# Hybrid encoder layer on one core: the sums of w_o planned behind the first output products, three more warm-up products, another transfer rate for the norm row

## The chip, the cores and the metric

The kernel runs on one core of a Trainium2 chip. The core has a matrix engine (TensorE, "PE" in the profile, with its weight loads as "PEld"), a vector engine (VectorE, DVE), a scalar engine (ScalarE, ACT), a general engine (GpSimd, POOL) and an engine that here only issues transfers (SyncE, SP). Each engine works through its own list of instructions in order; semaphores make one wait for another. The metric is the time on the device, in microseconds, of one execution; lower is better. Inputs and outputs lie in HBM.

## The reference

One layer over 512 tokens of width 1024, all in float32. Two sub-layers, each normed before and after:

```python
h = rmsnorm(x, pre_mix_norm)
proj = h @ w_in                       # z, x/B/C, dt, q, k, v, gates
y_ssd  = ssd_branch(z, xbc, dt, ...)  # conv, two scans, gated norm, @ w_ssd_out
y_attn = window_attention(q, k, v, sink, rel_table) @ w_attn_out
mixed = (g_ssd * y_ssd + g_attn * y_attn) @ w_o
x = x + rmsnorm(mixed, post_mix_norm)
f = square(relu(rmsnorm(x, pre_mlp_norm) @ w_mlp_in)) @ w_mlp_out
x = x + rmsnorm(f, post_mlp_norm)
```

The scan runs forward and backward over 8 groups of 4 heads, in chunks of 128 tokens. Its result is gated by silu(z), and normed within each group of 256 channels before `w_ssd_out` (2048 x 1024).

## The kernel before

**Arithmetic.** A float32 product is made of three faster ones: each operand is split into a high part `wh` (a cast on ACT) and a low part `wl` (source less high part, on POOL or DVE), and PE adds high by high, high by low and low by high. `mm3` issues the three. Weights come in chunks of 8 x 128 rows by 128 columns: SP fetches a chunk into `wr` (three buffers), ACT makes `wh` (three buffers), POOL `wl` (three buffers).

**Stages, in the order of the program.** A start of warm-up products on zeros (`WARM`), a broadcast of the first norm's gain by a one-row product (`pp<-g,one`), the norms and transposes of x, and the products for v and dt; then q, k, the gates, the eight scan groups (`ssd_quanta`, `ssd_steps`) with attention in between; then the output projection of the scan (`ssd_out_quanta`), the mix with w_o (`mix_quanta`), and the MLP.

**The turn from the scan to its output projection.** For the last group, `rms` sums the squares over partitions with two products against ones (operands `sh` and `sl`, the high and low part of the squares `ssq`), copies one row of the result (`rstd`), and sends it through HBM: row out (`rrow<-rstd`), back in as a column (`rcol<-rrow`), a power on POOL (`rsqrt_mean`, L383 and L385), out again (`rrow<-rcol`), and back as a row on all partitions (`rstd<-rrow`). DVE then makes the last two blocks of `yT` (L1179), which are split into `yh` and `yl` like the fourteen others (`split_y`, L1225 and L1226; eight of these lie in the tiles named `b`). `ssd_out_quanta` begins with the first fourteen blocks of y for the output columns 0 and 1 (`most`), and takes blocks 14 and 15 later (`rest`).

**The sums of w_o.** The mix is a product by halves in seven block products instead of eight, which needs sums of quarters of w_o. `stage_wo(k)`, for k from 0 to 3, fetches four tiles of w_o (L1341, tiles `wd`), makes four sums on DVE (L1344 to L1347) and stores them in HBM (L1349, tensors `wot`), from where the mix fetches them again (L1547). Here it is placed at the first quanta of the output projection: `c0 + STAGE + k` with STAGE at 0.

**What sets the order.** The program is written quantum by quantum (a quantum is one group of products, with side work put to it by `at`). At the end `chain` gives all instructions to `Planner`, which plays them through with durations of its own: an engine that is free takes, among the instructions that are ready, the one with the earliest deadline (PE the one that comes first in the program). The deadline of an instruction goes back from the PE instructions that need it. The order that comes out, engine by engine and for SP's transfers too, is fixed. `transfer` gives the planned length of a transfer by a rate for each source, and `COLD` the planned time up to which PE runs at half its pace. So a number in the planner moves instructions, and an engine in its fixed order waits where the plan was wrong.

Of the kernel before, what the change touches and what calls it, by code (L numbers as in the profile page):

```python
# [27 lines left out]

LO_MIX = "vp"
LO_DOWN = "p", "p", "p", "vp"  # L30
WARM = 10
LO_V = "pvpvpvpv"

SCAN = dict(load=3, weigh=(-2, -0.5), states=(0, 1), prep=(0, 1.5, 3, 4.5), outs=(2.5, 5.5), rms=9, finish=12,
            x_flip=2, b_flip=2)
LAST = dict(SCAN, prep=(0, 1, 3, 4), outs=(2.5, 5.5), rms=8, finish=10)
HEADS = dict(scores=0, flip=2, values=3.5)
FETCH, STAGE = 2, 0
BUCKET_STARTS = (1, 2, 3, 4, 5, 6, 7, 8, 12, 16, 23, 32, 46, 64, 91)


# [16 lines left out]
class Slots:  # L58


    def __init__(self, pool, n, tags):
        self.pool, self.free, self.slot, self.n, self.tags = pool, deque(range(n)), {}, 0, tags
# [14 lines left out]
class Planner:  # L77
# [10 lines left out]
    OVERLAP = {"ACT": 95, "DVE": 78, "POOL": 37, "PE": 0, "SP": 0}  # L88
    AFTER = {"ACT": 35, "DVE": 34, "POOL": 80, "PE": 53, "SP": 60}

    def __init__(self, instructions, tags):
        names = {"PE": "PE", "DVE": "DVE", "Activation": "ACT", "Pool": "POOL", "SP": "SP"}
        self.ins = [i for i in instructions if type(i).__name__ != "BassTilePoolBoundary"]
        self.eng = [names[str(i.engine).split(".")[-1]] for i in self.ins]
        self.tags = tags
        self.depend()
        self.cost = [self.duration(n) for n in range(len(self.ins))]
        self.kind = [self.matmul_kind(n) if e == "PE" else None for n, e in enumerate(self.eng)]

# [145 lines left out]
            late[n] = min([late[s] - self.AFTER[self.eng[s]] for s in self.post[n]] + [t + 5000.0]) - c  # L245
        return late

    COLD, LEAD, TAIL = 5300, 1000, 1300

    def transfer(self, n):  # L250

        dst, src = self.operands(self.ins[n].outs)[0], self.operands(self.ins[n].ins)[0]
        size = 4 * math.prod(d[1] for d in dst.ap)
        rows = {"csT": 120, "csE": 100, "in_w_in": 270, "in_w_mlp_in": 270, "in_w_ssd_out": 270, "in_w_attn_out": 270}
        return size / rows.get(src.tensor.name.rsplit("_", 1)[0] if src.tensor.name.startswith("cs") else src.tensor.name, 100 if size < 2 ** 17 else 310)

    def plan(self, wait=0.3):
        late = self.deadlines()
# [73 lines left out]
class Trunk:  # L332
    def __init__(self, ctx, tc, ins, out, dbg=None):
        self.tc, self.nc, self.out = tc, tc.nc, out
        self.__dict__.update({"d_" + k: v for k, v in ins.items()})
        self.d_w_in = ins["w_in"][0]
        self.dbg = dbg or {}
        pool = lambda name, **kw: ctx.enter_context(tc.tile_pool(name=name, bufs=1, **kw))
        self.cp = pool("cp")
        self.wp = pool("wp")  # L340
        self.sp = pool("sp")
        self.pm = pool("pm", space=PSUM)
        self.dp = pool("dp", space=DRAM)
        self.tags = {}
        self.slots = Slots(self.sp, SLOTS, self.tags)
        self.n = 0
        self.quanta, self.acts, self.now = [], {}, 0
        self.raw, self.parts, self.nraw, self.nspl, self.ring = {}, {}, 0, 0, set()

    def name(self, s):  # L350
# [138 lines left out]

    def chain(self):  # L490

        plan = Planner(self.nc.cur_bb.bb.instructions, self.tags)
        info = mybir.DependencyInfo(mybir.DependencyClass.NoSync, mybir.DependencyReason.DATA)
        for order in plan.plan().values():
            for a, b in zip(order, order[1:]):
                self.tc.add_manual_dep(plan.ins[b], plan.ins[a].name, info, reason="planned order")
# [823 lines left out]
    def load_x(self):  # L1320
# [7 lines left out]
        for t in range(NT):  # L1328
            self.x2[t] = [self.slots.get("x2") for _ in range(2)]
            for a, b in zip(self.x2[t], self.x1[t]):  # L1330
                self.nc.scalar.activation(a, b, AF.Copy, scale=self.rst0[:, t:t + 1])

    def stage_wo(self, k):

        nc = self.nc
# [309 lines left out]
    def build(self):  # L1645
# [6 lines left out]
        n = lambda: len(self.quanta)  # L1652
# [28 lines left out]
        c0 = n()  # L1681
        self.wot = {f"T{i}": self.dp.tile([512, 512], F32, name=f"wot{i}") for i in range(1, 5)}
        for k in range(4):
            self.at(c0 + STAGE + k, lambda k=k: self.stage_wo(k))
        self.at(c0, lambda: self.split_y(0, 14))
        self.add(*self.ssd_out_quanta())
        self.at(n() + 1, self.load_x)
# [44 lines left out]
```

## Time and profile before

| | us |
|---|---|
| runs shown (three): median, lowest, highest | 1089.49, 1088.82, 1089.90 |
| the profiled execution: its own time | 1092.5 |
| the profiled execution: its span | 1090.7 |

The page of the profile has the 40 slices of the span in these rows (busy tenths of each engine, granted PE clock, busy tenths of the DMA engines):

```profile
PE   9999999999999999999999999999999999999997
PEld 8788888888888888888888778888888888888885
DVE  5578887788796787886878863668863755665787
ACT  4567776686766768575677532475755534434443
POOL 3546567558558898999898866566998978978844
PEclk9999999999999999999999999999999999999999
DMA  6444524526435556555577964563721621621522
```

Each digit stands for 27 us. PE is at nine tenths or more up to the last slice; the other engines have room on the average. In the rows further on, "x <-y" in brackets behind an instruction says for how many us its engine stood idle before it, and what ended this; `L390` is the line of the helper `mm`, so that products are told apart by their tiles (`pp`, `ps` are banks of PSUM). "PEclk" is the granted clock as a share of the full one.

### The profile page before, as it was taken

What the parts mean: (1) busy time and instruction counts of PE and PEld (TensorE: products, weight loads), DVE (VectorE), ACT (ScalarE), POOL (GpSimd) and SP (SyncE); (2) the same over time, 40 slices, a digit from 0 to 9 for tenths busy, and PEclk for the clock granted to TensorE, in tenths of its full rate; (3) what the DMA queues carried; (4) which work ended last, traced back from release to release, by engine and by line L of the source; (5) the groups of instructions that cost most, each with busy time, mean ns of one, the idle gap of its engine ahead of it and who ended that gap; (6) DMA issues with size and microseconds to landing.
All of it is one profiled execution on the core that took longest, in us unless ns stands there. A gap on an engine that the chain in (4) does not pass through costs nothing.

```text
span 1090.7 us, 16951 instructions
## 1 busy us (share of the span) xinstructions
PE 1077.6 (99%) x5578; PEld 903.0 (83%) x5578; DVE 785.9 (72%) x1345; ACT 654.7 (60%) x1407; POOL 807.3 (74%) x1011
## 2 busy tenths in 40 slices
PE   9999999999999999999999999999999999999997
PEld 8788888888888888888888778888888888888885
DVE  5578887788796787886878863668863755665787
ACT  4567776686766768575677532475755534434443
POOL 3546567558558898999898866566998978978844
PEclk9999999999999999999999999999999999999999
DMA  6444524526435556555577964563721621621522
GB/s 204 127 124 121 152 75 121 147 67 164 128 112 159 152 144 164 156 150 163 141 188 207 284 176 134 162 225 112 246 66 53 191 69 52 192 65 57 161 93 78
DMA packets 221000, 152.21 MB, mean 140 GB/s; under 512 B 12494, under 2 KB 194230, under 8 KB 220913
## 3 DMA queue, kind: packets, MB, share of 16 engines
q1 hardware_dynamic: 220764, 151.06, 48.1%
q8 instruction: 44, 0.72, 0.3%
q14 instruction: 44, 0.35, 0.1%
q10 hardware_dynamic: 148, 0.07, 0.0%
HBM read 138.19 MB, written 12.91 MB: 139 GB/s over the span
## 4 chain that ended last, share of the span: by engine, by line
PE 92%; DVE 3%; DMA 2%; ACT 1%; issue 1%; POOL 0%; SPq 0%; POOLq 0%; DVEq 0%
PE pp L390 64%; PE ps L390 26%; PE ps L394 3%; DMA wr<-in_w_in 1%; DMA wd<-in_w_o 1%; DMA rstd<-rrow 1%; DVE wd L1345 0%; DMA rrow<-rcol 0%; ACT b L415 0%; DVE B L936 0%; DVE wd L1344 0%; DVE sl L408 0%; DVE x L1387 0%; DVE P L847 0%; DVE yT L1179 0%
## 5 line engine op out<-in xcount | busy, mean ns | idle before, releaser
L390 PE MATMUL pp<-b,wh 128*128 128x512 f32 (+1 forms) x1840 | 565.5, 388 | 0.2 <-DVE b L416 0.2
L469 POOL TENSOR_TENSOR wl<-wr,wh 128x256 fp32r<-128x256 f32 (+1 forms) x503 | 412.7, 849 | 140.0 <-ACT wh L465 129.9
L390 PEld LDWEIGHTS pp<-b,wh 128*128 128x128 f32 x1840 | 340.2, 188 | 67.9 <-issue 1.4
L390 PE MATMUL pp<-b,wl 128*128 128x512 f32 (+1 forms) x920 | 356.2, 387 | 0.0
L390 PEld LDWEIGHTS pp<-b,wl 128*128 128x128 f32 x920 | 172.8, 188 | 34.5
L465 ACT CAST wh<-wr 128x1024 fp32r<-128x1024 f32 x131 | 136.4, 1042 | 85.3 <-PE pp L390 68.0
L1561 POOL TENSOR_TENSOR wl<-wd,wh 128x256 fp32r<-128x256 f32 x168 | 139.3, 859 | 41.0 <-ACT wh L1557 35.2
L1557 ACT CAST wh<-wd 128x512 fp32r<-128x512 f32 x108 | 63.2, 618 | 55.0 <-PE pp L390 18.6
L390 PE MATMUL ps<-wh,fh 128*128 128x512 f32 (+1 forms) x196 | 75.5, 385 | 0.5 <-DVE acc L1607 0.5
L390 PE MATMUL ps<-wl,fh 128*128 128x512 f32 (+1 forms) x196 | 75.4, 385 | 0.0
L390 PE MATMUL ps<-wh,fl 128*128 128x512 f32 (+1 forms) x196 | 75.4, 385 | 0.0
L1104 ACT ACTIVATE n<-cb,tables 128x128 f32<-128x128 f32 x128 | 49.2, 391 | 18.2 <-DVE cb L1095 15.8
L1435 DVE SCALAR_TENSOR_TENSOR pp<-pp,r 128x512 f32<-128x512 f32 (+1 forms) x31 | 17.5, 566 | 56.0 <-ACT r L1432 55.9
L1561 POOL TENSOR_TENSOR wl<-wt,wh 128x256 fp32r<-128x256 f32 x56 | 45.4, 846 | 9.9 <-ACT wh L1557 6.0
L1140 POOL TENSOR_TENSOR w<-w,E 128x256 f32<-128x256 f32 x48 | 42.3, 893 | 11.8 <-DVE w L1136 5.4
L936 DVE SCALAR_TENSOR_TENSOR u<-pp,cv,u 128x510 f32<-128x510 f32 (+1 forms) x64 | 47.7, 745 | 3.4 <-ACT u L932 2.1
L1034 POOL TENSOR_TENSOR xd<-x,tables 128x256 f32<-128x256 f32 x48 | 35.5, 757 | 18.3 <-ACT x L959 16.0
L1105 ACT ACTIVATE m<-cb,tables 128x128 f32<-128x128 f32 x128 | 48.9, 388 | 0.0
L1100 ACT ACTIVATE rf<-rf,tables 128x128 f32<-128x128 f32 x128 | 42.4, 393 | 5.0 <-DMA rf<-csT 5.0
L390 PEld LDWEIGHTS ps<-wh,fh 128*128 128x128 f32 x196 | 36.8, 188 | 8.0 <-DVE acc L1607 0.7
L856 ACT ACTIVATE P<-P,mx 128x384 f32<-128x384 f32 (+1 forms) x64 | 35.2, 552 | 13.5 <-DVE mx L853 8.4
L390 PEld LDWEIGHTS ps<-wh,fl 128*128 128x128 f32 x196 | 36.8, 188 | 7.4
(301 smaller groups left out, 2094.5 us busy)
## 6 DMA issues: line engine op xcount, KB each, us to landing
wr<-in_w_in SPq DMA_DIRECT2D x74, 512.0 KB, 4.2
wr<-in_w_mlp_in SPq DMA_DIRECT2D x32, 512.0 KB, 4.1
wd<-in_w_mlp_out SPq DMA_DIRECT2D x64, 256.0 KB, 4.7
rb<-csT SPq DMA_DIRECT2D x32, 256.0 KB, 3.2
rf<-csT SPq DMA_DIRECT2D x32, 256.0 KB, 5.2
wd<-in_w_o SPq DMA_DIRECT2D x28, 256.0 KB, 4.7
wr<-in_w_ssd_out SPq DMA_DIRECT2D x14, 512.0 KB
E<-csE SPq DMA_DIRECT2D x96, 64.0 KB, 4.3
```

The lines of the kernel that those rows point to most:

```text
L390: self.nc.tensor.matmul(out, lhsT, rhs, start=start, stop=stop, skip_group_check=more)
L465: self.nc.scalar.copy(hi[:, :m], raw)
L469: engines[e].tensor_tensor(lo[:, c], raw[:, c], hi[:, c].bitcast(F32), op=ALU.subtract)
L856: nc.scalar.activation(p[:, :w], p[:, :w], AF.Exp, bias=mx[:, n:n + 1], accum_out=sm[:, n:n + 1])
L936: nc.vector.scalar_tensor_tensor(u[:, a:e], ps[:, a + d:e + d], self.wtap(t, b), u[:, a:e], op0=ALU.mult, op1=ALU.add)
L1034: nc.gpsimd.tensor_tensor(v4(xd[:, d * 256:(d + 1) * 256]), v4(xs(c)), by_dir(self.coef, c)[:, d].unsqueeze(2).to_broadcast([128, 4, 64]), ...
L1100: nc.scalar.activation(v4(rf)[:, h], v4(rf)[:, h], AF.Identity, bias=ncs[:, 0, h:h + 1])
L1104: nc.scalar.activation(v4(n)[:, h], cb[:, 0], AF.Copy, scale=dt[:, 0, h:h + 1])
L1105: nc.scalar.activation(v4(m)[:, h], cb[:, 1], AF.Copy, scale=dt[:, 1, h:h + 1])
L1140: nc.gpsimd.tensor_tensor(wc, wc, E[:, d], op=ALU.add)
L1557: nc.scalar.copy(hi, w)
L1561: (nc.vector if e == "v" else nc.gpsimd).tensor_tensor(low[:, q], w[:, q], hi[:, q].bitcast(F32), op=ALU.subtract)
```

## The change

It has three parts. `WARM` goes from 10 to 13 products, each of which is two PE instructions, and `COLD` from 5300 to 5600. STAGE goes from 0 to 1, and everything that `stage_wo` issues, its transfers too, is noted as held back: in the planner such an instruction may not begin before the PE instruction that stands last ahead of it in the program has begun. It is a rule for the plan alone; no semaphore is added. And transfers from `rrow` are planned at 70 instead of 100.

```diff
--- before.py
+++ after.py
@@ -28,14 +28,14 @@
 
 LO_MIX = "vp"
 LO_DOWN = "p", "p", "p", "vp"
-WARM = 10
+WARM = 13
 LO_V = "pvpvpvpv"
 
 SCAN = dict(load=3, weigh=(-2, -0.5), states=(0, 1), prep=(0, 1.5, 3, 4.5), outs=(2.5, 5.5), rms=9, finish=12,
             x_flip=2, b_flip=2)
 LAST = dict(SCAN, prep=(0, 1, 3, 4), outs=(2.5, 5.5), rms=8, finish=10)
 HEADS = dict(scores=0, flip=2, values=3.5)
-FETCH, STAGE = 2, 0
+FETCH, STAGE = 2, 1
 BUCKET_STARTS = (1, 2, 3, 4, 5, 6, 7, 8, 12, 16, 23, 32, 46, 64, 91)
 
 
@@ -88,12 +88,19 @@
     OVERLAP = {"ACT": 95, "DVE": 78, "POOL": 37, "PE": 0, "SP": 0}
     AFTER = {"ACT": 35, "DVE": 34, "POOL": 80, "PE": 53, "SP": 60}
 
-    def __init__(self, instructions, tags):
+    def __init__(self, instructions, tags, held=()):
         names = {"PE": "PE", "DVE": "DVE", "Activation": "ACT", "Pool": "POOL", "SP": "SP"}
         self.ins = [i for i in instructions if type(i).__name__ != "BassTilePoolBoundary"]
         self.eng = [names[str(i.engine).split(".")[-1]] for i in self.ins]
         self.tags = tags
         self.depend()
+        last = None
+        for n, i in enumerate(self.ins):
+            if self.eng[n] == "PE":
+                last = n
+            elif i.name in held:
+                self.turn[n].add(last)
+                self.next[last].append(n)
         self.cost = [self.duration(n) for n in range(len(self.ins))]
         self.kind = [self.matmul_kind(n) if e == "PE" else None for n, e in enumerate(self.eng)]
 
@@ -245,14 +252,14 @@
             late[n] = min([late[s] - self.AFTER[self.eng[s]] for s in self.post[n]] + [t + 5000.0]) - c
         return late
 
-    COLD, LEAD, TAIL = 5300, 1000, 1300
+    COLD, LEAD, TAIL = 5600, 1000, 1300
 
     def transfer(self, n):
 
         dst, src = self.operands(self.ins[n].outs)[0], self.operands(self.ins[n].ins)[0]
         size = 4 * math.prod(d[1] for d in dst.ap)
-        rows = {"csT": 120, "csE": 100, "in_w_in": 270, "in_w_mlp_in": 270, "in_w_ssd_out": 270, "in_w_attn_out": 270}
-        return size / rows.get(src.tensor.name.rsplit("_", 1)[0] if src.tensor.name.startswith("cs") else src.tensor.name, 100 if size < 2 ** 17 else 310)
+        rows = {"rrow": 70, "csT": 120, "csE": 100, "in_w_in": 270, "in_w_mlp_in": 270, "in_w_ssd_out": 270, "in_w_attn_out": 270}
+        return size / rows.get(src.tensor.name.rsplit("_", 1)[0].rstrip("01234567") if src.tensor.name.startswith(("cs", "rrow")) else src.tensor.name, 100 if size < 2 ** 17 else 310)
 
     def plan(self, wait=0.3):
         late = self.deadlines()
@@ -345,6 +352,7 @@
         self.slots = Slots(self.sp, SLOTS, self.tags)
         self.n = 0
         self.quanta, self.acts, self.now = [], {}, 0
+        self.late = set()
         self.raw, self.parts, self.nraw, self.nspl, self.ring = {}, {}, 0, 0, set()
 
     def name(self, s):
@@ -489,7 +497,7 @@
 
     def chain(self):
 
-        plan = Planner(self.nc.cur_bb.bb.instructions, self.tags)
+        plan = Planner(self.nc.cur_bb.bb.instructions, self.tags, self.late)
         info = mybir.DependencyInfo(mybir.DependencyClass.NoSync, mybir.DependencyReason.DATA)
         for order in plan.plan().values():
             for a, b in zip(order, order[1:]):
@@ -1330,6 +1338,12 @@
             for a, b in zip(self.x2[t], self.x1[t]):
                 self.nc.scalar.activation(a, b, AF.Copy, scale=self.rst0[:, t:t + 1])
 
+    def held_back(self, fn):
+
+        n = len(self.nc.cur_bb.bb.instructions)
+        fn()
+        self.late |= {i.name for i in self.nc.cur_bb.bb.instructions[n:]}
+
     def stage_wo(self, k):
 
         nc = self.nc
@@ -1681,7 +1695,7 @@
         c0 = n()
         self.wot = {f"T{i}": self.dp.tile([512, 512], F32, name=f"wot{i}") for i in range(1, 5)}
         for k in range(4):
-            self.at(c0 + STAGE + k, lambda k=k: self.stage_wo(k))
+            self.at(c0 + STAGE + k, lambda k=k: self.held_back(lambda: self.stage_wo(k)))
         self.at(c0, lambda: self.split_y(0, 14))
         self.add(*self.ssd_out_quanta())
         self.at(n() + 1, self.load_x)
```

What the planner makes of it is seen in three places. Lines of the changed kernel are 8 to 14 higher than before (L408 is L416 there, L1226 is L1234, L1344 to L1347 are L1358 to L1361, L445 is L453, L375 is L383).

On DVE, at the turn to the output projection. `wd` are tiles of w_o and their sums, `sl` is the low part of the last group's squares, `yl` and `b` are low parts of y. Before:

```order
L1226 TENSOR_TENSOR yl_7241<-yT_3605,yh_7240 128x512
L1345 TENSOR_TENSOR wd_7500<-wd_7494,wd_7492 128x512
L1347 TENSOR_TENSOR wd_7496<-wd_7496,wd_7500 128x512
L1344 TENSOR_TENSOR wd_7427<-wd_7431,wd_7427 128x512
L1345 TENSOR_TENSOR wd_7433<-wd_7427,wd_7425 128x512
L1347 TENSOR_TENSOR wd_7429<-wd_7429,wd_7433 128x512
L1346 TENSOR_TENSOR wd_7434<-wd_7431,wd_7433 128x512
L1344 TENSOR_TENSOR wd_7346<-wd_7350,wd_7346 128x512
L1226 TENSOR_TENSOR yl_7245<-yT_3608,yh_7244 128x512
L1345 TENSOR_TENSOR wd_7352<-wd_7346,wd_7344 128x512
L408 TENSOR_TENSOR sl_7121<-ssq_6934,sh_7120 128x512
L1226 TENSOR_TENSOR b_7230<-yT_5059,b_7228 128x512
```

In the changed kernel:

```order
L1234 TENSOR_TENSOR yl_7230<-yT_3611,yh_7229 128x512
L1234 TENSOR_TENSOR yl_7238<-yT_4451,yh_7237 128x512
L1144 TENSOR_TENSOR w_6510<-ps_7103,w_6510 128x512
L416 TENSOR_TENSOR sl_7124<-ssq_6937,sh_7123 128x512
L1234 TENSOR_TENSOR b_7215<-yT_5062,b_7213 128x512
L1234 TENSOR_TENSOR b_7215<-yT_5065,b_7213 128x512
```

and, behind the eight splits into `b`, in the changed kernel:

```order
L1234 TENSOR_TENSOR b_7216<-yT_6896,b_7214 128x512
L1358 TENSOR_TENSOR wd_7331<-wd_7335,wd_7331 128x512
L1187 SCALAR_TENSOR_TENSOR yT_7430<-w_6500,cv,rstd_7264 128x256
L1187 SCALAR_TENSOR_TENSOR yT_7430<-w_6510,cv,rstd_7264 128x256
L1187 SCALAR_TENSOR_TENSOR yT_7433<-w_6500,cv,rstd_7264 128x256
L1187 SCALAR_TENSOR_TENSOR yT_7433<-w_6510,cv,rstd_7264 128x256
L1359 TENSOR_TENSOR wd_7337<-wd_7331,wd_7329 128x512
L1234 TENSOR_TENSOR yl_7437<-yT_7430,yh_7436 128x512
L1234 TENSOR_TENSOR yl_7441<-yT_7433,yh_7440 128x512
L1360 TENSOR_TENSOR wd_7338<-wd_7335,wd_7337 128x512
```

`sl` has no sum of w_o ahead of it any more; before it had 13 of the 16. The first sum now stands directly ahead of the last group's `yT`, the next two behind it.

On SP, the transfers of the last group's norm row (`rrow`, `rcol`, `rstd`), among fetches of output weights (`wr`), of attention gates (`gate<-gd`), of w_o and stores of its sums. Before:

```order
L445 DMA wr_7208<-in_w_ssd_out 128x2x256
L915 DMA gate_7585<-gd 128x512
L1167 DMA rcol_7281<-rrow_7282 128x4
L445 DMA wr_7340<-in_w_ssd_out 128x8x128
L445 DMA wr_7342<-in_w_ssd_out 128x8x128
L915 DMA gate_7660<-gd 128x512
L1169 DMA rrow_7282<-rcol_7281 128x4
L1349 DMA wot_70<-wd_7501 128x512
L1547 DMA wd_7928<-in_w_o 128x512
L1349 DMA wot_73<-wd_7348 128x512
L1349 DMA wot_70<-wd_7353 128x512
L375 DMA rstd_7279<-rrow_7282 128x512
```

In the changed kernel:

```order
L1174 DMA rrow_7267<-rstd_7264 1x512
L1175 DMA rcol_7266<-rrow_7267 128x4
L453 DMA wr_7325<-in_w_ssd_out 128x8x128
L923 DMA gate_7588<-gd 128x512
L1177 DMA rrow_7267<-rcol_7266 128x4
L453 DMA wr_7327<-in_w_ssd_out 128x8x128
L1355 DMA wd_7331<-in_w_o 128x512
L1355 DMA wd_7335<-in_w_o 128x512
L383 DMA rstd_7264<-rrow_7267 128x512
L1355 DMA wd_7329<-in_w_o 128x512
L1355 DMA wd_7333<-in_w_o 128x512
L453 DMA wr_7406<-in_w_ssd_out 128x8x128
```

The column of the norm row goes out again (`rrow<-rcol`) one weight fetch earlier, and behind it stand a weight fetch and two fetches of w_o where three stores of sums and a fetch for the mix stood. All sixteen fetches and stores of `stage_wo` now come among the output weights that follow; before, most of them were ahead of the first row here.

In the start, on DVE: `b` are low parts of the normed and transposed x, `wv` low parts of the first weights. Before:

```order
L408 TENSOR_TENSOR b_168<-ps_184,b_166 128x4x128
L408 TENSOR_TENSOR b_167<-ps_202,b_165 128x4x128
L573 TENSOR_TENSOR wv_116<-wr_108,wv_115 128x320
L408 TENSOR_TENSOR b_168<-ps_210,b_166 128x4x128
L573 TENSOR_TENSOR wv_127<-wr_123,wv_126 128x320
L573 TENSOR_TENSOR wv_135<-wr_123,wv_134 128x320
```

In the changed kernel:

```order
L416 TENSOR_TENSOR b_171<-ps_187,b_169 128x4x128
L581 TENSOR_TENSOR wv_119<-wr_111,wv_118 128x320
L581 TENSOR_TENSOR wv_130<-wr_126,wv_129 128x320
L416 TENSOR_TENSOR b_170<-ps_205,b_168 128x4x128
L416 TENSOR_TENSOR b_171<-ps_213,b_169 128x4x128
L581 TENSOR_TENSOR wv_138<-wr_126,wv_137 128x320
```

Two splits of weights move ahead of the `b` of the second tile of x. On SP, in the start: `wr` are the first weight chunks of the input projection, `cst` the constants, the others small vectors. Before:

```order
L664 DMA v_56_492<-in_ssd_norm 16x128
L445 DMA wr_217<-in_w_in 128x8x128
L665 DMA v_56_492<-in_pre_mlp_norm 8x128
L375 DMA dtb<-in_a_log 128x64
L375 DMA sink<-in_attn_sink 128x16
L445 DMA wr_226<-in_w_in 128x8x128
L445 DMA wr_235<-in_w_in 128x8x128
L625 DMA cst<-in_cst 128x384
L375 DMA dsk_593<-in_d_skip 128x32
```

In the changed kernel:

```order
L453 DMA wr_220<-in_w_in 128x8x128
L672 DMA v_56_495<-in_ssd_norm 16x128
L673 DMA v_56_495<-in_pre_mlp_norm 8x128
L383 DMA dtb<-in_a_log 128x64
L383 DMA sink<-in_attn_sink 128x16
L633 DMA cst<-in_cst 128x384
L383 DMA dsk_596<-in_d_skip 128x32
L453 DMA wr_229<-in_w_in 128x8x128
L453 DMA wr_238<-in_w_in 128x8x128
```

The first weight chunk moves one row up, and the constants and `dsk` move ahead of the next two chunks. On PE the three further warm-up products stand with the ten, ahead of the broadcast of the gain.

## The prediction

> **What bounds the kernel now.** I read the page first (the chain that ended last), then busy time by stretches, then the timeline of each engine around the one stretch where TensorE (PE) stops.
>
> ```profile
> span 1090.7 us, 16951 instructions
> ...
> PE 92%; DVE 3%; DMA 2%; ACT 1%; issue 1%; POOL 0%; SPq 0%; POOLq 0%; DVEq 0%
> ...
> 30.00:619.50 589.50, 589.39 (x3321) 495.17 (x3320) 463.61 (x826) 412.07 (x957) 442.81 (x543) 1.00 0.53 146
> 619.50:647.40 27.90, 25.00 (x101) 19.54 (x100) 17.86 (x17) 9.70 (x15) 17.98 (x16) 0.94 0.80 229
> 624.70:628.20 3.50, 3.50 (x11) 2.71 (x10) 3.50 (x5) 1.68 (x3) 1.75 (x1) 0.51 0.78 250
> 647.40:700.00 52.60, 52.60 (x233) 43.51 (x232) 27.92 (x38) 16.49 (x23) 33.30 (x42) 1.00 0.42 126
> ```
>
> After its clock comes the stretch's length, then busy time of PE, PEld, DVE, ACT, POOL, then granted clock, DMA share and GB/s. From 30 to 619.5 us PE is busy 589.39 of 589.50 us: moving other engines' work there can gain nothing. In 619.5 to 647.4 it is busy only 25.0 of 27.9, and for 3.5 us of that the granted clock is 0.51. That stretch is the turn from the last gate products to the scan's output projection, and the edit that holds the w_o sums back acts exactly there.
>
> ```profile
> 619.53 0.39 PE L390 MATMUL ps<-sh,ones_r 128*128 128x512 f32 x1
> ...
> 620.98 0.50 PE L390 MATMUL pp<-yh,wl 128*128 128x512 f32 x1 [0.60 <-POOL wl L469]
> ...
> 623.75 0.50 PE L390 MATMUL ps<-sl,ones_r 128*128 128x512 f32 x1 [1.81 <-DVE sl L408]
> ...
> 646.81 0.73 PE L390 MATMUL pp<-yh,wh 128*128 128x512 f32 x2 [0.50 <-ACT yh L1225]
> ...
> 723.52 5.44 PE pp L390 x24
> ```
>
> Undisturbed, 24 products of 512 columns take 5.44 us, 0.227 each. The program has 98 products from the one at 619.53 to the one at 646.81: 22.2 us at that pace, against 27.28. So **5.06 us are lost here**: 0.60 + 1.81 + 0.50 of waits, about 1.7 in the slow-clock stretch (3.5 us at 0.51 of the pace), the rest in refilling after each wait. The longest wait is for sl, the low half of the last group's sum of squares, on DVE:
>
> ```profile
> 613.00 1.06 DVE L1345 TENSOR_TENSOR wd<-wd,wd 128x512 f32<-128x512 f32 x1
> ...
> 618.59 2.88 DVE L1345 TENSOR_TENSOR wd<-wd,wd 128x512 f32<-128x512 f32 x1
> 621.39 2.30 DVE L408 TENSOR_TENSOR sl<-ssq,sh 128x512 fp32r<-128x512 f32 x1
> ...
> 616.99 0.62 ACT L407 CAST sh<-ssq 128x512 fp32r<-128x512 f32 x1 [0.52 <-POOL ssq L1148]
> ...
> 605.90 5.92 DMA wd<-in_w_o
> ```
>
> Its operands are there at 617.6 (616.99 + 0.62), but DVE takes a w_o sum first (618.59, 2.88 us), and the chain of waits runs on back through the sums to a fetch of w_o that took 5.92 us. **PE waits for w_o sums that nothing needs yet.**
>
> **The change part by part.** *Sums held back.* Of the 16 sums of w_o 13 stand ahead of sl on DVE before, none now:
>
> ```profile
> L1345 DVE TENSOR_TENSOR wd<-wd,wd 128x512 f32<-128x512 f32 x4 | 6.3, 1569 | 0.1
> ...
> L1347 DVE TENSOR_TENSOR wd<-wd,wd 128x512 f32<-128x512 f32 x4 | 5.8, 1449 | 0.1
> L1344 DVE TENSOR_TENSOR wd<-wd,wd 128x512 f32<-128x512 f32 x4 | 4.7, 1185 | 1.5 <-DMA wd<-in_w_o 1.5
> ...
> L1346 DVE TENSOR_TENSOR wd<-wd,wd 128x512 f32<-128x512 f32 x4 | 3.3, 817 | 0.0
> ```
>
> They are 20.1 us of DVE in all. Without them sl can start at 617.6. At its present 2.30 us it ends at 619.9, where PE wants it at 619.76 (it is now the product right behind the one at 619.53): a wait of 0.2 to 0.4 at most; and with POOL less disturbed, ssq itself is earlier, so I take none. The 0.60 on POOL's split of the first output weights should go too: POOL does the same operations ahead of it, with fewer two-input sums of DVE among them. With these two waits goes their consequence, the slow clock. What is late next is the norm row of the last group, which feeds yh:
>
> ```profile
> 624.29 0.58 ACT L1162 COPY rstd<-ps 1x512 f32<-1x512 f32 x1 [2.38 <-PE ps L390]
> ...
> 626.31 0.33 SPq L1167 DMA_DIRECT2D rcol<-rrow  x1
> ...
> 633.09 0.52 POOL L383 TENSOR_SCALAR rcol<-rcol 128x4 f32<-128x4 f32 x1
> ...
> 635.05 3.17 DMA rrow<-rcol
> 638.28 5.81 DMA rstd<-rrow
> ...
> 580.37 0.37 SPq L1167 DMA_DIRECT2D rcol<-rrow  x1
> ...
> 584.93 0.30 POOL L383 TENSOR_SCALAR rcol<-rcol 128x4 f32<-128x4 f32 x1 [0.30 <-DMA rcol<-rrow]
> ```
>
> From the sl product (623.75) to yh's product (646.81) it takes 23.1 us. It will begin 4.0 earlier, at 619.76. POOL now has the norm row ahead of a weight split; the step from the fetch of rcol to POOL, 6.8 us (626.31 to 633.09), should shrink to about the 4.6 of the group before (580.37 to 584.93, where POOL waited for that DMA): 2.2 saved. Against it, SP now issues a weight fetch and two w_o fetches ahead of the broadcast of rstd, and DVE makes one held sum (1.2 us, from its row) ahead of yT; I put 0 to 2.2 on these. So yh is ready 20.9 to 23.1 us after 619.76, at 640.7 to 642.9. PE, with 94 products before it, comes there at 619.53 + 94 x 0.227 = 640.9. The wait is 0 to 2.0; I take 0.5, as now, since the two additions overlap DMAs that are under way. **Gain of the stage: 5.06 - 0.5 = 4.5 us**; at best 5.06, at worst 5.06 less 2.0 here, 0.4 at sl and 1.7 for a slow clock that returns, 1.0.
>
> *What the sums meet where they go.* Sixteen fetches, sixteen stores and 20 us of DVE move into 630 to 700 us. From 647.4 DVE is busy 27.9 of 52.6 us and the DMA share is 0.42, so there is room; PE is busy throughout, and its cover is the three-deep weight buffers (weighed under the rivals). POOL pays:
>
> ```profile
> 592.16 4.51 POOL L469 TENSOR_TENSOR wl<-wr,wh 128x256 fp32r<-128x256 f32 x4 [0.77 <-ACT wh L465]
> ...
> 664.75 2.83 POOL L469 TENSOR_TENSOR wl<-wr,wh 128x256 fp32r<-128x256 f32 x4 [1.50 <-ACT wh L465]
> ```
>
> Four pieces of a split take 2.83 us where DVE is nearly idle and 4.51 among the sums, 0.42 more a piece. Sixteen sums that each lengthen one piece so add 6.7 us to POOL's 33.3 of 52.6; were POOL to stand still for all 20.1 us of them, it would be 53.4 of 52.6, full. So the cost to PE is 0 to 0.8 us. I take 0, as even 4.51 is under the 5.44 us in which PE uses a chunk of weights. [...]
>
> *Warm-up.* Three more products, six instructions:
>
> ```profile
> 1.04 4.63 PE L390 MATMUL ps<-zero 128*128 128x128 f32 x20 [1.04 <-DVE zero L552]
> 5.60 3.78 PE L390 MATMUL pp<-g,one 1*128 1x512 f32 x4
> 9.31 2.08 PE L390 MATMUL ps<-zero 128*128 128x128 f32 x8
> 11.18 2.74 PE L394 MATMUL ps<-ident,junk 128*128 128x128 f32 x12
> ...
> 14.63 0.60 PE L394 MATMUL ps<-ident,junk 128*128 128x128 f32 x4
> ...
> 15.41 0.68 DVE b L408
> 16.09 0.85 DVE wv L573
> ...
> 18.97 6.97 DMA wr<-in_w_in
> ...
> 27.82 3.98 PE ps L390 x24
> ```
>
> 20 take 4.63 us, so six are 1.39 us. They are on the chain that ended last: warm-up, row broadcast (pp<-g), transposes, cast, DVE's wv (16.09), which frees a buffer for the fetch at 18.97, on which PE waits at 27.8. In the other direction, DVE now makes that wv ahead of the b at 15.41, so 0.68 earlier. PE runs at half pace until about 13.7 (twelve transposes in 2.74, later four in 0.60); if the longer warm-up brings full pace before the broadcast, this takes about 1.9 instead of 3.78. So the front is worth +1.4 (nothing helps) to -1.2 (1.39 - 1.9 - 0.68). SP's new order (the constants ahead of two weight fetches) lies in between. I take 0, the middle, since no row decides.
>
> *Rate of the norm row, COLD.* These only reorder 220 to 600 us a little, behind a PE that is busy all the time: 0, plus or minus 0.3.
>
> **Sum.** 1092.5 us of the profiled execution (span 1090.7, and 1.8 around it) less 4.5 is 1088.0. The runs shown have a median of 1089.49, 3.0 less than the profiled one; I carry the difference over: 1089.49 - 4.5 = **1085.0**.
>
> **The rivals.** *The norm row becomes the wait:* the full 2.0 us at yh, 0.4 at sl, and a slow-clock stretch of 1.7 again: gain 1.0, 1088.5. For it: three DMAs in a row, each with 3 to 6 us, and w_o fetches that still go ahead of the broadcast. Against it: POOL's step is freed.
>
> *Full clock early:* the front gives 1.2 more, 1083.8. For it: full pace came at 13.7, 4.4 us after the dense products resumed at 9.31, and 6.0 us of dense warm-up are longer than that; against it: the present 4.56 us (1.04 to 5.60) did not do. [...]
>
> *Slower, through SP's queue:* SP issues in order, and a store of a sum stands ahead of the next output-weight fetch. The store waits for its sum, and this for a w_o fetch:
>
> ```profile
> wr<-in_w_in SPq DMA_DIRECT2D x74, 512.0 KB, 4.2
> ...
> 639.59 1.05 ACT L465 CAST wh<-wr 128x1024 fp32r<-128x1024 f32 x1 [1.87 <-PE pp L390]
> ```
>
> Three buffers of 5.44 us are 16.3 us from release to reuse; a fetch (4.2, as for the input weights), a cast (1.05) and a split at its slowest (4.51) leave 6.5 us. A set that holds SP for its fetch (5.92) and two sums (3.1) holds it 9.0: 2.5 us of PE, four times, 10.0, less 4.5: 5.5 slower, 1095.0. It decides as soon as SP is held over 6.5 us behind a store. Against it: in the new order most fetches of a set go out before the store of the set ahead, and SP waits there for a weight buffer anyway.
>
> *Nothing moves:* the stall is in the profiled execution alone, whose 3.0 us above the median are of its size; 1089.5.
>
> **How the numbers follow.** Forecast 0.55; early clock 0.15; norm row 0.17; SP 0.08; nothing 0.05. 0.2% (2.2 us) is about what a measurement of this kernel tells from no change. Faster by over that: forecast, early clock, and 0.04 of the norm row (where it waits less): 0.74. Within: the other 0.13 and nothing: 0.18. Slower: 0.08. The range reaches from 1083.2 (5.06 and a front of -1.2) to 1088.5, which leaves out 0.13.
>
> **What would show it.** Right: in 619 to 625 us no PE wait on sl, granted clock 1.00 throughout, a rstd broadcast issued some 6 us earlier than 638.28, w_o sums between 635 and 690 with PE busy. Wrong: a PE wait on yh of over 1 us, a stretch at half clock behind it, PE waits on wl or wh between 647 and 710, or a start in which the first product with wv is later than 13.6 by over 1 us.

## The result, and the profile after

| | before | after |
|---|---|---|
| runs, one after the other on one chip (six each): median | 1089.99 | 1085.35 |
| lowest to highest | 1088.82 to 1091.52 | 1084.97 to 1085.44 |
| the profiled execution: its time (span) | 1092.5 (1090.7) | 1085.44 (1083.7) |

All times in us. The ratio after to before is 0.9956, 95% interval 0.9943 to 0.9969: faster by 4.64 in the medians. The spans of the two profiled executions differ by more, 7.0.

The page of the kernel after, span and chain that ended last, and its busy time by stretches (length, busy PE, PEld, DVE, ACT, POOL, granted clock, DMA share, GB/s), the same stretches as before:

```profile
span 1083.7 us, 16956 instructions
...
PE 94%; DVE 2%; DMA 2%; ACT 1%; SPq 1%; issue 1%; POOL 0%; POOLq 0%; DVEq 0%
```

```profile
28.40:619.50 591.10, 591.02 (x3326) 496.20 (x3325) 451.07 (x819) 413.38 (x960) 438.96 (x544) 1.00 0.50 135
619.50:647.40 27.90, 27.90 (x125) 23.08 (x124) 15.46 (x18) 10.07 (x14) 17.51 (x16) 1.00 0.68 209
624.70:628.20 3.50, 3.50 (x17) 2.92 (x16) 0.00 (x0) 0.34 (x2) 2.45 (x2) 1.00 0.72 216
647.40:700.00 52.60, 52.60 (x234) 43.57 (x233) 41.38 (x53) 17.50 (x28) 39.59 (x42) 1.00 0.87 280
```

PE is busy 27.90 of 27.90 where it was busy 25.00, at full clock, and stays busy behind it, where the sums now run (DVE 41.4 instead of 27.9, DMA share 0.87 instead of 0.42). The timeline of the kernel after, engines together, at the same turn (start, length, engine, operation, in brackets the idle time ahead of it and what ended it):

```profile
610.35 0.62 ACT L415 CAST sh<-ssq 128x512 fp32r<-128x512 f32 x1 [0.84 <-POOL ssq L1156]
611.01 2.92 DVE L416 TENSOR_TENSOR sl<-ssq,sh 128x512 fp32r<-128x512 f32 x1 [5.88 <-ACT sh L415]
...
618.29 0.40 PE L398 MATMUL ps<-sl,ones_r 128*128 128x512 f32 x1
...
620.54 0.35 SPq L1175 DMA_DIRECT2D rcol<-rrow  x1
...
623.39 0.52 POOL L391 TENSOR_SCALAR rcol<-rcol 128x4 f32<-128x4 f32 x1
...
628.70 0.43 SPq L383 DMA_DIRECT2D rstd<-rrow  x1
...
633.89 0.69 DVE L1358 TENSOR_TENSOR wd<-wd,wd 128x512 f32<-128x512 f32 x1 [9.44 <-DMA wd<-in_w_o]
634.61 0.33 SPq L1363 DMA_DIRECT2D wot<-wd  x1
635.72 2.82 DVE L1187 SCALAR_TENSOR_TENSOR yT<-w,cv,rstd 128x256 f32<-128x256 f32 x4 [1.13 <-DMA rstd<-rrow]
638.58 1.13 ACT L1233 CAST yh<-yT 128x512 fp32r<-128x512 f32 x2
639.42 0.62 PE L398 MATMUL pp<-yh,wh 128*128 128x512 f32 x2
```

`sl` is ready at 613.93 (611.01 + 2.92), 4.4 ahead of its product. The first of the two casts of `yh` ends near 639.2, half of 1.13 behind its start, and the product that needs it, the 94th behind `sh`'s (618.06), starts at 639.42: only 0.2 in hand. So of the three waits and the half-clock stretch at the turn nothing is left.

Then the start. PE's timeline of the kernel after:

```profile
1.04 5.50 PE L398 MATMUL ps<-zero 128*128 128x128 f32 x26 [1.04 <-DVE zero L560]
6.46 1.98 PE L398 MATMUL pp<-g,one 1*128 1x512 f32 x4
...
26.16 3.79 PE L398 MATMUL ps<-wv,b 128*128 128x320 f32 x24 [0.93 <-ACT b L415]
```

The row broadcast takes 1.98 instead of 3.78, so PE was at the quicker pace already. The eight products on zeros behind it take 1.20 instead of 2.08, and the longer warm-up costs 0.87 (5.50 against 4.63): 1.8 in all, and the first product with `wv` starts 1.82 earlier (11.78 instead of 13.60). The pace does not last. By stretches, before and after:

```profile
9.00:14.00 5.00, 5.00 (x23) 4.69 (x23) 3.78 (x7) 1.73 (x5) 1.54 (x4) 1.00 0.92 267
```

```profile
9.00:14.00 5.00, 5.00 (x31) 4.95 (x31) 5.00 (x10) 3.78 (x12) 3.17 (x6) 0.66 0.99 285
```

The granted clock after is 0.66 here, and the twelve transposes take 2.77, as slow as before (2.74, where the row says 1.00; more on that in the last section). PE goes on at 26.16, before at 27.82: 1.66 earlier. With the 5.06 of the turn that is 6.7 of the 7.0 between the two spans. The medians differ by 4.64 only, so either the turn or the start of these two executions is not that of the others. The experiments take the parts one by one.

### The profile page after: what moved, and what is told of

It reads as the page before. It is cut to its first block, busy times and chain, and to the rows that moved or that the text cites. A ratio compares the mean times of both kernels' runs of the same rounds, so it can differ in the third digit from the quotient of the medians.

```text
span 1083.7 us, 16956 instructions
## 1 busy us (share of the span) xinstructions
PE 1073.5 (99%) x5584; PEld 902.2 (83%) x5584; DVE 785.1 (72%) x1345; ACT 654.4 (60%) x1407; POOL 808.1 (75%) x1011
## 4 chain that ended last, share of the span: by engine, by line
PE 94%; DVE 2%; DMA 2%; ACT 1%; SPq 1%; issue 1%; POOL 0%; POOLq 0%; DVEq 0%
PE pp L398 66%; PE ps L398 25%; PE ps L402 3%; DMA x<-in_x 1%; DMA wr<-in_w_in 0%; ACT b L423 0%; DVE B L944 0%; DVE x L1401 0%; DVE P L855 0%; DVE x L1655 0%; DVE acc L1621 0%; SPq L383 0%; SPq L570 0%; DVE Q L832 0%; DVE ag L1648 0%
## 5 line engine op out<-in xcount | busy, mean ns | idle before, releaser
L477 POOL TENSOR_TENSOR wl<-wr,wh 128x256 fp32r<-128x256 f32 (+1 forms) x503 | 418.2, 860 | 137.4 <-ACT wh L473 133.9
L398 PEld LDWEIGHTS ps<-wl,fh 128*128 128x128 f32 x196 | 36.8, 188 | 7.4
```

The source lines that it names most:

```text
L398: self.nc.tensor.matmul(out, lhsT, rhs, start=start, stop=stop, skip_group_check=more)
L477: engines[e].tensor_tensor(lo[:, c], raw[:, c], hi[:, c].bitcast(F32), op=ALU.subtract)
```

## The experiments

The three parts in all combinations, each in five rounds (the kernel before has 24 to 32 runs beside each set, medians 1089.94 to 1090.93):

| held back, STAGE 1 | new rate | 13 products | median | lowest to highest (runs) | ratio, 95% interval |
|---|---|---|---|---|---|
| | | | 1090.54 | 1086.64 to 1093.77 (24) | 1 |
| x | | | 1086.95 | 1086.03 to 1087.94 (10) | 0.9967 (0.9957 to 0.9978) |
| | x | | 1087.08 | 1085.45 to 1088.38 (7) | 0.9969 (0.9956 to 0.9982) |
| | | x | 1088.96 | 1087.54 to 1093.38 (12) | 0.9994 (0.9981 to 1.0008) |
| x | x | | 1085.57 | 1085.40 to 1087.31 (5) | 0.9960 (0.9944 to 0.9975) |
| x | | x | 1085.78 | 1085.33 to 1088.39 (12) | 0.9953 (0.9935 to 0.9970) |
| | x | x | 1085.87 | 1084.63 to 1087.77 (11) | 0.9955 (0.9940 to 0.9971) |
| x | x | x | 1085.35 | 1084.97 to 1085.44 (6) | 0.9956 (0.9943 to 0.9969) |

The medians are from three sets of runs and the one of the result; the ratios are each to the runs of before in the same set, and need not be the ratio of two medians of this table. The single parts and the pair of held sums and rate ran on one chip, the other two pairs each on another, so a comparison across sets is also one across chips.

**Sums held back alone.**

```diff
 in the change:
-WARM = 13
+WARM = 10
-    COLD, LEAD, TAIL = 5600, 1000, 1300
+    COLD, LEAD, TAIL = 5300, 1000, 1300
-        rows = {"rrow": 70, "csT": 120, ...
+        rows = {"csT": 120, ...
```

> The held-back sums alone (STAGE at 1, ten warm-up products and the old planned rates as before). Theory A, the turn: the whole gain is the 5.06 us that TensorE lost between the products at 619.5 and 646.8 us; alone it gives the 4.6 us of the whole change, from 4.3 to 5.1, and the trace has no wait of TensorE on sl and a granted clock of 1.00 from 619.5 to 647.4 us. Rival B, the front: the trace after resumed at 26.16 us after the first fetch, 1.66 earlier than before; if that is in every execution, this kernel gains only 4.64 - 1.66 = 3.0. Rival C, the rate: the rstd row comes late without the new rate, a wait on yh of over 1 us comes back, and the gain is under 3.5.

Measured: 1086.95, 3.6 under the 1090.54 beside it. PE's timeline and DVE's have `sl` ready at 615.95 for a product at 619.78:

```profile
613.04 2.91 DVE L416 TENSOR_TENSOR sl<-ssq,sh 128x512 fp32r<-128x512 f32 x1 [6.42 <-ACT sh L415]
...
619.78 0.40 PE L398 MATMUL ps<-sl,ones_r 128*128 128x512 f32 x1
```

The stall is gone, but the gain lies between theory A (4.3 to 5.1) and rival B (3.0). Rival C's gain of under 3.5 is just missed, and there is no wait on `yh`. Its start is the slow one (broadcast 3.78).

**Warm-up alone.**

```diff
 in the kernel before:
-WARM = 10
+WARM = 13
-    COLD, LEAD, TAIL = 5300, 1000, 1300
+    COLD, LEAD, TAIL = 5600, 1000, 1300
```

> Three more warm-up products (and the planned cold time of 5600) alone. Theory A: 0, from -0.7 to +0.7 us, because what the trace after shows at the front (clock up before the row broadcast, TensorE resuming 1.66 us earlier) is not in every execution. Rival B: 1.4 to 2.0 us faster in the median, with the row broadcast in about 2.0 us instead of 3.78 and the first product with wv near 11.8 us instead of 13.6. Rival D: 1.0 to 1.4 slower, if the added 1.39 us is paid and the clock comes no earlier. In all three the 5.06 us at the turn stay lost.

Measured: 1088.96, 1.6 lower in the median; the ratio's interval includes no change. So this run does not part A from B by time. Its trace shows the quick broadcast of B and the turn's stall as before, without the half-clock stretch. PE's timeline in the start and its waits, then the turn's stretches:

```profile
6.88 2.00 PE L398 MATMUL pp<-g,one 1*128 1x512 f32 x4
...
26.36 3.78 PE L398 MATMUL ps<-wv,b 128*128 128x320 f32 x24 [1.10 <-ACT b L415]
```

```profile
PE ps L398 <- DVE sl L416: 1.8, 1, 1.8
...
PE pp L398 <- POOL wl L477: 0.6, 1, 0.6
```

```profile
620.00:624.00 4.00, 2.19 (x10) 1.58 (x9) 4.00 (x5) 1.62 (x4) 1.51 (x1) 1.00 1.02 331
624.00:628.00 4.00, 4.00 (x20) 3.30 (x19) 4.00 (x4) 1.59 (x2) 2.78 (x2) 1.00 0.54 165
```

The same waits, 0.6 and 1.8, and the clock stays at 1.00. Before, the granted clock fell to 0.51 behind them. **So these waits alone do not bring the half-clock stretch.** With one profiled execution of each kernel it is not shown what else decides. The span is 1086.7. The kernel with the same warm-up, the new rate and no stall (further down; PE goes on at 26.15 there) has a span of 1083.7; 0.2 of the difference lies in the start, so at full clock the turn costs some 2.8, not 5.06.

**The rate alone.**

```diff
 in the kernel before:
-        rows = {"csT": 120, ...
+        rows = {"rrow": 70, "csT": 120, ...
```

> The new planned rate of the norm row alone. Theory A: within 0.3 us of before; 11 of the 16 sums of w_o still stand ahead of sl, so the wait of TensorE on sl stays at 1 to 2 us. Rival C: the reordered row helps by itself, over 1 us faster. Rival E: the reordering of the scan groups costs, over 1 us slower, with TensorE waits between 220 and 600 us that the trace before does not have.

Measured: 1087.08, 3.5 under before: as much as the held sums. Theory A and rival E fall; C was right that it helps by itself, though not through the norm row. DVE's and PE's timeline:

```profile
617.01 2.89 DVE L416 TENSOR_TENSOR sl<-ssq,sh 128x512 fp32r<-128x512 f32 x1
...
620.05 0.40 PE L398 MATMUL ps<-sl,ones_r 128*128 128x512 f32 x1
```

Eleven sums of w_o still stand ahead of `sl`, but the one of 2.88 that started at 618.59 before, directly ahead of it, is behind it now. `sl` is ready at 619.90, 0.15 ahead of its product; PE's weight load for it waited 0.17 for `sl`, so nothing more than that is in hand. That the reordering of the sums does it is read from the trace; no run moves that one sum alone.

**Without the warm-up.**

```diff
 in the change:
-WARM = 13
+WARM = 10
-    COLD, LEAD, TAIL = 5600, 1000, 1300
+    COLD, LEAD, TAIL = 5300, 1000, 1300
```

> The change without its three warm-up products: sums held back and new rate, ten warm-up products. Theory A: the whole gain of 4.6 us, from 4.3 to 5.1, and the same as with the sums held back alone within 0.5. Rival B, the front: 3.0 us, 1.66 less than the whole change. Rival D: 0.5 to 1.4 us more gain than the whole change, if its longer warm-up is paid in most executions.

Measured: 1085.57 from five runs, three within 0.2 of each other and two higher (1086.38, 1087.31). In the profiled execution the quick broadcast came with ten products too (2.06):

```profile
1.04 4.63 PE L398 MATMUL ps<-zero 128*128 128x128 f32 x20 [1.04 <-DVE zero L560]
5.60 2.06 PE L398 MATMUL pp<-g,one 1*128 1x512 f32 x4
...
25.91 4.01 PE L398 MATMUL ps<-wv,b 128*128 128x320 f32 x24 [0.85 <-ACT b L415]
```

The whole gain is there, as A said, but it is 1.4 better than the held sums alone, more than A's 0.5. If the early clock came in some of the five runs only, as it did in the profiled one, that leaves open how much of that the rate makes.

**Without the rate.** (In the change, the row of `rrow` taken out of `rows`.)

> The change without the new rate: sums held back and thirteen warm-up products. Seen so far: with ten products the row broadcast of the start takes 3.78 us in three profiled executions (TensorE resumes at 27.4 to 27.8 us) and 2.06 in one (25.9); with thirteen 1.98 and 2.00 in both (26.2 and 26.4). Theory F, the parts: the front is worth 1.2 to 1.7 us in the executions whose clock came late, thirteen products make it early in all, and the rate adds nothing to held sums. Then this kernel stands at 1085.1 to 1085.7 with a spread of its runs under 1 us, and its first broadcast takes about 2 us. Rival C, the rate: what divides 1086.95 (held sums alone) from 1085.57 (with the rate) is the rate; then this kernel stays at 1086.5 to 1087.3.

Measured: 1085.78, twelve runs, eleven of them between 1085.33 and 1086.36 and one at 1088.39. Theory F holds for the size and for the broadcast (1.98); 0.1 high in the median, and one run out of its spread. Rival C falls. Three more products gain 1.2 here (from 1086.95), and 1.2 beside the rate (1087.08 to 1085.87), both across chips; the ratios, to the runs of before on the same chip, differ by 0.0014 each time, or 1.5. Beside both other parts they gain 0.2 (1085.57 to 1085.35).

**Warm-up without the new order of the start.**

```diff
 in the change:
-    COLD, LEAD, TAIL = 5600, 1000, 1300
+    COLD, LEAD, TAIL = 4500, 1000, 1300
```

> The change with the planned cold time at 4500 in place of 5600. The thirteen warm-up products stay, but the transfers of the start stand nearly as before: the constants and dsk behind the two weight chunks again, and one of the two early weight splits back behind a b. Theory F, the products make the clock come early: 1085.1 to 1085.8, no other than the whole change, spread under 1 us. Rival G, the order of the start brings it: 1086.5 to 1087.3, as with the sums held back alone.

**Ten products, the start planned nearly as in the change.**

```diff
 in the change:
-WARM = 13
+WARM = 10
-    COLD, LEAD, TAIL = 5600, 1000, 1300
+    COLD, LEAD, TAIL = 6500, 1000, 1300
```

> The change with ten warm-up products, and the planned cold time at 6500, so that the transfers and weight splits of the start stand nearly as in the whole change. Theory F, two parts: ten products catch the early clock in some executions only (two of five profiled so far), so the runs fall in two groups, near 1085.0 to 1085.6 and near 1086.3 to 1087.3, with a spread over 1.2 us; median 1085.4 to 1087.0. Rival G, the order of the start does it all: one group, spread under 1 us, median 1085.0 to 1085.6.

These two belong together. The first: 1086.86, in two groups (1085.41 to 1086.49, 1087.23 to 1088.93); the second: 1088.58 (1086.87 to 1090.19). The first lies in rival G's range and is slower than F, but its profiled broadcast is quick (1.98) all the same, and its runs are in two groups; the second is slower than either theory allows. Both have a wait that the change doesn't have. From the second's timeline of SP, DVE and PE:

```profile
19.27 4.65 SPq L383 DMA_DIRECT2D dsk<-in_d_skip  x1
...
27.53 1.36 DVE L651 COPY dcol<-dsk 64x16 f32<-64x16 f32 x2 [4.56 <-DMA dsk<-in_d_skip]
...
29.07 1.28 DVE L416 TENSOR_TENSOR b<-ps,b 128x512 fp32r<-128x512 f32 x2
29.80 1.45 PE L398 MATMUL ps<-wv,b 128*128 128x320 f32 x8 [0.88 <-DVE b L416]
```

In both kernels `dsk`, a transfer of 16 KB, stands behind two weight chunks on SP, and its copy on DVE stands ahead of the `b` that PE needs. Here SP takes 4.65 to issue it. In the change it stands ahead of the chunks:

```profile
17.97 0.94 SPq L383 DMA_DIRECT2D dsk<-in_d_skip  x1
```

The copies are then over at 23.03 (22.03 + 1.00). So the order of the start counts as well. A late `dsk` alone isn't the fault: before, it goes out at 24.28, but there only one of the two copies stands ahead of that `b` (28.26, 0.27 long), and PE has no wait on it.

**STAGE at 1, nothing held.**

```diff
 in the change:
-            self.at(c0 + STAGE + k, lambda k=k: self.held_back(lambda: self.stage_wo(k)))
+            self.at(c0 + STAGE + k, lambda k=k: self.stage_wo(k))
```

> The change with STAGE at 1 but the sums not held back in the plan: 8 of the 16 sums stand ahead of sl again (13 before, 11 with the rate alone), all 16 ahead of the last yT. Theory H, only the time on DVE decides: sl is ready at about 617 to 619 us, just ahead of its product, as with the rate alone (ready 619.9, wanted 620.05); no wait of TensorE on sl, 1085.1 to 1085.8, as the whole change. Rival I, any sum ahead of sl costs: a wait of 0.5 to 2 us on sl, and 1086.5 to 1089 us.

Measured: 1085.33, the same as the change; theory H holds, rival I falls. So beside the other two parts and STAGE at 1, the rule that holds the sums back adds nothing that these runs can tell. Eight sums stand ahead of `sl`, and it is ready at 617.18 (614.74 + 2.44), its product at 618.44.

**Only the last set of sums held.**

```diff
 in the kernel before, with held_back:
-            self.at(c0 + STAGE + k, lambda k=k: self.stage_wo(k))
+            self.at(c0 + STAGE + k, lambda k=k: self.held_back(lambda: self.stage_wo(k)) if k == 3 else self.stage_wo(k))
```

> The kernel before with only the last of the four sets of sums held back (STAGE at 0, ten warm-up products, old rates): 10 sums ahead of sl instead of 13, one of them still directly ahead of it. Theory H, only the time on DVE decides: three sums of 1.2 us less put sl 3 us or more earlier, its wait of 1.81 us goes, and the time is that of the held sums alone, 1086.5 to 1087.5. Rival J, the sum directly ahead of sl (2.88 us) or the fetch of w_o that it follows makes the wait: it stays at 1 us or more, and the time at 1089 to 1091.

Measured: 1087.51 (1086.39 to 1094.34), at H's upper end, with a longer tail, but not by H's account. The wait on `sl` falls from 1.81 to 0.39 and isn't gone, and the norm row comes up as the next wait; the profiled execution makes up for it with a quick broadcast (1.98). PE's timeline:

```profile
619.14 0.50 PE L398 MATMUL ps<-sl,ones_r 128*128 128x512 f32 x1 [0.39 <-DVE sl L416]
...
639.57 0.96 PE L398 MATMUL pp<-yh,wh 128*128 128x512 f32 x3 [1.24 <-ACT yh L1233]
```

**Sixteen products.** (In the change, WARM at 16 and COLD at 5900.)

> The change with sixteen warm-up products in place of thirteen (planned cold time 5900). Theory F: with thirteen the clock already came in front of the row broadcast in all five profiled executions, so six more instructions buy nothing and cost at most their own time at full pace, 6 x 0.15 (eight took 1.16 to 1.20 us) = 0.9 us: 1085.3 to 1086.3. Rival K, the phase is still a matter of chance with thirteen: sixteen make the runs more even and lower, 1084.4 to 1085.1.

Measured: 1086.33 (1085.42 to 1089.76), 1.0 worse; rival K falls, F is exceeded by little. Four of the twelve runs are at 1087.8 and above; what happens in those stays open. The profiled one shows why nothing is gained:

```profile
26.36 3.78 PE L398 MATMUL ps<-wv,b 128*128 128x320 f32 x24 [1.60 <-ACT b L415]
```

The broadcast takes 1.98, as with thirteen, and PE waits for the same `b`.

**Rate and warm-up, no sums held.** (In the change, STAGE at 0 and no `held_back`.)

> The change without its first part: thirteen warm-up products and the new rate, sums of w_o where the plan puts them (STAGE at 0, none held back; 11 ahead of sl, all 16 ahead of the last yT). Theory H: as the rate alone already brought sl in time (ready 619.9, wanted 620.05), holding back is not needed: 1085.1 to 1085.9, no wait on sl over 0.3 us. Rival L: with only 0.15 us in hand the stall returns in part of the executions: 1086.0 to 1088.0 with a spread of 2 us or more.

Measured: 1085.87, inside H, but from 1084.63 to 1087.77, as L said of the spread. In the profiled execution `sl` is ready at 618.34 (615.45 + 2.89), its product at 618.51: 0.17 in hand, and the weight load waited 0.15 for it. The two highest runs (1087.69, 1087.77) are 1.8 to 1.9 above the median, less than the 2.8 of the whole stall; whether it comes back there was not seen.

**Two quanta further.** (In the change, STAGE at 3.)

> The change with STAGE at 3: held back two quanta further, no fetch of w_o ahead of the broadcast of rstd and no sum ahead of the last yT (two and one in the change). Theory M, TensorE is covered on both sides: within 0.4 us of the change, 1085.0 to 1085.8, with no wait on yh, wl or wh. Rival N, the queue of SP: the sums come closer to the mix that needs them, stores hold up fetches of output weights, waits on wl or wh between 640 and 720 us, 1 to 5 us slower. Rival O, the 0.2 us in hand at yh is too little in part of the executions of the change: 0.3 to 0.5 faster.

Measured: 1085.19 (1084.88 to 1085.49): theory M. Rival N falls, PE has no wait on `wl` or `wh`; O's 0.3 isn't reached. The stretch in which the sums run is full here too:

```profile
647.40:700.00 52.60, 52.60 (x233) 43.57 (x233) 40.38 (x52) 17.26 (x27) 36.88 (x39) 1.00 0.93 298
```

Its runs overlap with those of the change, so it is no faster by what these can tell.

## Why the prediction was right, and where its terms were not

1085.0 was forecast, 1085.35 measured. That it came out within 0.4 is in part luck: two terms erred in opposite directions, held sums by -0.9 and warm-up by up to +1.2.

**Sums held back, forecast 4.5.** The mechanism was right in each step on the way to the profiled execution: no wait on `sl`, none on the first output weights, full clock (1.00), and the norm row is late next. From `sl`'s product (618.29) to `yh` (639.2) it takes 20.9, the lower end of the 20.9 to 23.1; the 0.5 kept for `yh` was not paid, by a margin of 0.2. From the fetch of `rcol` to POOL it takes 2.85 (620.54 to 623.39) where 4.6 was put. The broadcast of `rstd` goes out at 628.70 instead of 638.28, 9.6 earlier, not 6; 1.5 of it is the earlier start (`sh`'s product at 618.06 instead of 619.53). In the profiled execution all of the 5.06 came back. The size was wrong in the median: alone, the part gains 3.6. The step that failed is "I carry the difference over": it took the 3.0 between the profiled execution and the median to lie elsewhere, with the whole 5.06 in every execution. But some 2 of the 5.06 is the half-clock stretch and what follows it: with the same two waits (0.6 and 1.8) the warm-up-only kernel ran on at a granted clock of 1.00 and lost 2.8. So the slow clock is not simply "their consequence", as the forecast had it: the wait on `sl` is 1.8 in both profiles, the clock 0.51 in one and 1.00 in the other. The wait and the clock should have been two terms. The mean granted clock of the single runs speaks for this: 3.5 us at half clock lower it by 0.0016 (1.75 of 1087), and of the twelve runs of the warm-up alone the four slowest (1090.94 and above) have 0.994 or 0.995, the six fastest (1088.51 and below) 0.996 to 0.998. In which stage those four lost it is not on record, and what divides the two traces, 0.51 and 1.00, no run here shows.

**POOL beside the moved sums, forecast 0.** 6.7 us of lengthening were forecast for 647 to 700; POOL's busy time there went from 33.30 to 39.59, 6.3 more, and PE is busy 52.60 of 52.60. The cover of three weight buffers held. The 0.8 at the other end of the forecast, for a POOL that stands still for all 20.1 of the sums, was not paid: four pieces of a split took 2.82 to 4.71 there, under the 5.44 in which PE uses a chunk.

**Warm-up, forecast 0.** Wrong by about 1.2 beside one other part, by 0.2 beside both: the rival "full clock early" is what happened, beside the forecast (1.98 for the broadcast instead of 3.78), though the clock did not stay (0.66 from 9 to 14 us in the change). In the profiled executions the broadcast took about 2.0 in all eight kernels with thirteen or sixteen products, and in two of six with ten (3.78 in the other four). The chance is not settled by so few, but the medians go the same way in all four pairs (1.6, 1.2, 1.2 and 0.2). Three of the four pairs are across sets, and the runs of the two kernels overlap in each, least in the second. The two kernels with ten products, held sums and the old order of the start show how it reaches PE. SP's and ACT's timelines, first with the slow broadcast (held sums alone), then with the quick one (held sums and rate):

```profile
17.02 0.40 SPq L453 DMA_DIRECT2D wr<-in_w_in  x1
18.98 1.31 SPq L453 DMA_DIRECT2D wr<-in_w_in  x2
...
25.53 1.05 ACT L473 CAST wh<-wr 128x1024 fp32r<-128x1024 f32 x1 [2.17 <-DMA wr<-in_w_in]
```

```profile
15.64 0.40 SPq L453 DMA_DIRECT2D wr<-in_w_in  x1
17.60 1.44 SPq L453 DMA_DIRECT2D wr<-in_w_in  x2
...
24.05 1.05 ACT L473 CAST wh<-wr 128x1024 fp32r<-128x1024 f32 x1 [2.49 <-DMA wr<-in_w_in]
```

The fetches go out 1.38 earlier, the cast starts 1.48 earlier, and PE, which waits for the `b` behind that cast on ACT, goes on at 25.91 instead of 27.39. The bounds of +1.4 to -1.2 held, but for the 1.6 of the warm-up alone, which is not clear of noise; taking their middle "since no row decides" gave both ends the same weight, where the end with the early clock is the one that came. That the order of the start has a price of its own wasn't seen: with ten products, held sums and the rate, the new order with `dsk` late stands 3.0 above the old one (1088.58 against 1085.57, twelve runs and five). The two ran on different chips. The trace shows 0.88 of that as the wait behind `dsk`, and the slow broadcast makes another part. Seven of the twelve runs have a mean granted clock of 0.993 to 0.995, none of the five (0.996 to 0.998), so half-clock time may be a third part; where it lies stays open.

**Rate of the norm row, forecast 0 plus or minus 0.3.** The worst-sized term. Alone it gains 3.5: "these only reorder 220 to 600 us a little" left out that a plan that shifts earlier also moves what stands ahead of `sl` at 618. It doesn't show in the sum, because the rate and the held sums take away the same stall: 3.6 and 3.5 alone, 1085.78 with the first and 1085.35 with both beside thirteen products.

**The rivals.** The norm row as the new wait did not come in the change, by 0.2; with only the last set held it did, with 1.24. SP's queue did not decide: the first store goes out at 634.61, 4.2 behind the weight fetch ahead of it (630.43) and within the 6.5 from which it would decide, and PE waits for no weights behind it, also with STAGE at 3. That the stall is in the profiled execution alone falls with the 3.6 of the held sums; for the half-clock part of it the thought was right.

**What makes the runs of the change so even** (0.47 from lowest to highest over six runs, against 2.70 among the six of before beside them) was not taken apart fully. Three things that may vary from run to run are out: the slow broadcast (1.98 in its profile), the thin margin at `sl` (4.4 against 0.15 with the rate alone), the half clock behind the stall (1.00 from 619.5 to 647.4). They are not the whole of it: with the same start (1.98) and as wide a margin (4.2), one of the twelve runs without the rate is at 1088.39.

## What to carry to other kernels

Where a plan sets the order, price an edit by what it moves at the stalls that bound the kernel, not by what it is named for: a rate for a small transfer took the same sum out of the way as the rule made for it, and the gains of the parts alone (3.6, 3.5 and 1.6, the last not clear of noise) do not add to the 4.6 of the whole. When the profiled execution is well above the median, split its stall into the waits and the half-clock time behind them, and don't count the second for every execution: here the same waits had a clock of 0.51 behind them in one profile and 1.00 in the other. A wait removed by 0.15 us and one removed by 4.4 us look the same in one profile; the margin is in the operand's ready time and in the wait of the weight load.

## What the runs showed of the hardware that was not expected

The granted clock of the profile does not show the slow start. From 6 to 9 us the kernel with the held sums alone, whose broadcast products take 3.78, and the one with the warm-up alone (2.00) have these rows by stretches, the first and then the second:

```profile
6.00:9.00 3.00, 3.00 (x4) 0.77 (x3) 1.39 (x3) 1.45 (x4) 0.91 (x3) 1.00 1.06 352
```

```profile
6.00:9.00 3.00, 3.00 (x10) 1.53 (x10) 1.00 (x3) 1.05 (x3) 0.23 (x2) 1.00 1.00 345
```

Both say 1.00, while the same four products last 3.78 in the one and 2.00 in the other. In the start the pace has to be read from the products' own durations.

Nor does a quick broadcast mean that the clock stays. In eight of the ten profiled executions with one, the granted clock has a mean of 0.94 over the first 28 us (28.4 in the change). In the change it is at 0.50 from 10 to 12 us, and its mean from 7 to 13.2 us is 0.72: 3.5 us at half clock (6.2 x 0.28 / 0.50), as long as the stretch at the turn before. The warm-up alone and the sixteen products show 1.00 over the first 28 us. None of the four with the slow broadcast shows a fall in the record (1.00 over the first 28 or 30 us), but their transposes are slow as well (2.58 to 2.77 for twelve in three of them). What decides it is not shown.
